# A transformer block on one core: where the second norm's factor enters, how wide the w_ada sums are, and when they run

## The chip, the core and the metric

One core of a Trainium2 chip runs the whole kernel. The time is device microseconds of one execution, the median of three runs. Engines are named as in the profile: PE multiplies matrices, PEld loads its stationary operand, DVE is the vector engine, ACT the scalar engine, POOL and SP here mostly issue transfers.

## What is computed

One block with batch 1, 256 rows (SEQ), 2048 columns (D), everything in float32:

```python
mod = silu(c) @ w_ada + b_ada                      # 6 vectors of 2048
sh1, sc1, g1, sh2, sc2, g2 = split(mod, 6)
h = rms_norm(x, norm_mix_g) * (1 + sc1) + sh1
u, q, k, v, ga, gb = split(h @ w_in)               # 8192 columns
merged = sigmoid(ga) * (s5(u) @ w_proj_ssm) + sigmoid(gb) * (attention(q, k, v) @ w_proj_attn)
x = x + g1 * (merged @ w_out)
h2 = rms_norm(x, norm_mlp_g) * (1 + sc2) + sh2
x = x + g2 * (square(relu(h2 @ w_ff1)) @ w_ff2)    # 8192 hidden
return rms_norm(x, norm_final_g)
```

`s5` is a state-space scan over the rows with a GLU (`w_glu`) behind it.

## The kernel before

**Weights.** Each float32 product is made of three products of a shorter type (hi by hi, hi by lo, lo by hi). Weights come in 456 tiles of 128x1024 (512 KB): `load` (L133 to L141) issues the transfer on SP into one of seven `wraw` buffers, and `split` (L143) makes the high part `whi` by an ACT cast (L145) and the low part `wlo` by a DVE subtract (L147), each with four buffers. In order: 80 tiles of w_in for q, k, v and u, woven with the first groups of the gate columns; 48 for the gates `ga`, `gb`; 8 of w_proj_attn, 8 of w_glu, 8 of w_proj_attn, 16 of w_proj_ssm, 32 of w_out, then ff1 and ff2. `stream` hands the tiles to three forms of product: `gemm_t` (L177 to L179, 24 matmuls of 128x256 a tile, transposed result `pt`), `gemm_d` (L194 and L196, result `pd`) and `gemm_n` (L218 to L220, 12 of 128x512, result `pn`). Matmul results share five banks ("mm"), small ones three ("ax").

**Side work.** After each weight tile `step` runs the jobs of the lanes, each lane with a rate in jobs per tile (R1, R2, RS0, RWO, RM and so on). The order on each engine is then set by a scheduler that simulates the program; `hot` and high priority move parts of it ahead, and `after` keeps an instruction behind another one. The lane that matters here is "ada": the vectors of `mod` are row sums of the transposed w_ada times silu(c). One sum is a load of 128x1024 and one DVE instruction with an accumulator (L279). The scale and shift of the first norm come first: 48 such sums for rows 4 to 15 of its 16 (`mod1`, into a ring of `ahm` tiles), in pairs of 128-row blocks, each pair with its part of the normed input (`make_h1`: `htmp`, `ah`) behind it. Next come 96 sums, "late", for the second norm's scale and shift (A2, B2) and the gate g1, through the `wraw` buffers; last 32 for g2 during ff1 and ff2.

**Attention and scan.** When u is complete it goes over POOL's queue into another layout (`hop_in`, L743), and POOL then loads the table `tz` of attention's position terms (L441). Attention's first step on DVE reads scores and `tz` (`ga<-sco,tz`, L694). Scan and gating follow in lane "m".

**The second norm.** Behind w_out, four banks at a time are multiplied by g1 (L1168), added to x (L1169) and squared with a sum on ACT (L1170); L1185 and L373 to L378 give the factor `rs2` of each row. `scale2` multiplies x by it (L1177, L1180), `make_h` transposes (`trh`, L669), applies A2 and B2 on ACT (`htmp`, L681) and splits into `h2h`. The first four units g of ff1 (`pt`, 1024 columns each) start with the first half of the rows (8 tiles by `gemm_t`), whose results ACT copies into `part` (L1282); the second half is added by `gemm_d`, and ReLU, square and split follow (L1229, L1230).

## Time and profile before

| what | value |
|---|---|
| median of three runs | 1422.48 us (1420.78 to 1424.05) |
| the profiled execution | 1422.84 us |
| its span | 1421.0 us |
| PE busy | 1376.6 us (97%) |
| DVE busy | 1057.4 us (74%) |
| ACT busy | 700.4 us (49%) |
| transfers | 354.52 MB, mean 249 GB/s |

A span is from the first to the last instruction; the rest of the execution lies around it. Matmuls are pipelined, so a PE that is called busy can still be fed slowly, and the time lost is best read from the distance of one matmul's start to the next. Rows of the timeline give start and duration in us, engine, line, operation, output and input tiles, and in brackets the idle time before it and what ended it.

### The profile page before, as it was taken

The page shows a single profiled execution, that of the slowest core. Times are in us where ns is not written, and L with a number is a line of the kernel's source. Part 1 is how long each engine was busy: PE and PEld are TensorE (multiplying, and loading weights), DVE is VectorE, ACT ScalarE, POOL GpSimd, SP SyncE. Part 2 cuts the span into 40 slices and gives each one's busy share as a digit, 9 for nine tenths or more (in the row PEclk, how much of TensorE's full clock was granted, in tenths as well). Part 3 has the DMA queues.
Part 4 walks back from the last instruction along what each step waited for, and adds up shares of the span by engine and source line. Part 5 has one row for each costly group of instructions (what it writes and reads, how often), then busy time and mean ns, then how long its engine had stood idle before and what let it go on. Part 6 is the DMA issues. An engine that isn't in the chain of part 4 may idle for free.

```text
span 1421.0 us, 24325 instructions
## 1 busy us (share of the span) xinstructions
PE 1376.6 (97%) x9716; PEld 1245.0 (88%) x9716; DVE 1057.4 (74%) x1517; ACT 700.4 (49%) x919; POOL 42.5 (3%) x95
## 2 busy tenths in 40 slices
PE   6999989999999999999899999999999999999996
PEld 5899989989899999988799988888888888888885
DVE  5798998876899788977686686778666555555676
ACT  4554434346645743345555554635363544634444
POOL 1000000400002200000000000000000000000000
PEclk9999999999999999999899999999999999999998
DMA  9999965795447999787598568788778666566551
GB/s 372 408 376 327 317 228 174 228 298 193 140 161 245 320 336 321 290 332 258 183 344 291 176 230 255 257 231 328 203 275 264 214 191 193 177 207 191 181 206 60
DMA packets 111346, 354.52 MB, mean 249 GB/s; under 512 B 12176, under 2 KB 12208, under 8 KB 110816
## 3 DMA queue, kind: packets, MB, share of 16 engines
q1 hardware_dynamic: 108336, 347.13, 71.9%
q0 software_dynamic: 2896, 5.83, 1.4%
q8 instruction: 76, 1.25, 0.4%
q14 instruction: 38, 0.31, 0.1%
HBM read 348.70 MB, written 2.51 MB: 247 GB/s over the span
## 4 chain that ended last, share of the span: by engine, by line
PE 87%; DVE 6%; DMA 3%; ACT 2%; issue 2%; SPq 0%; DVEq 0%; ACTq 0%
PE pd L194 12%; PE pn L218 11%; PE pn L219 11%; PE pn L220 11%; PE pt L177 11%; PE pt L178 10%; PE pt L179 10%; PE pd L196 6%; DVE wlo L147 2%; DMA wraw<-in_w_in_dram 2%; DVE wraw L279 1%; ACT whi L145 1%; PE trv L603 1%; DMA wraw<-in_w_proj_attn_dram 1%; PE rk L637 1%
## 5 line engine op out<-in xcount | busy, mean ns | idle before, releaser
L145 ACT CAST whi<-wraw 128x1024 fp32r<-128x1024 f32 x456 | 473.8, 1050 | 574.2 <-PE pt L178 189.5
L147 DVE TENSOR_TENSOR wlo<-wraw,whi 128x1024 fp32r<-128x1024 f32 x456 | 553.7, 1224 | 268.6 <-ACT whi L145 261.8
L194 PE MATMUL pd<-h2h,whi 128*128 128x512 f32 x768 | 265.9, 395 | 0.4 <-DVE part L1224 0.4
L177 PE MATMUL pt<-ah,whi 128*128 128x256 f32 x896 | 252.2, 289 | 10.2 <-ACT ah L145 8.1
L178 PE MATMUL pt<-ah,whi 128*128 128x256 f32 x896 | 252.9, 286 | 0.0
L179 PE MATMUL pt<-ah,wlo 128*128 128x256 f32 x896 | 246.7, 286 | 6.2 <-DVE wlo L147 6.2
L196 PE MATMUL pd<-h2h,wlo 128*128 128x256 f32 x768 | 208.1, 279 | 0.0
L219 PE MATMUL pn<-whi,ff 128*128 128x512 f32 x512 | 199.3, 389 | 0.0
L218 PE MATMUL pn<-whi,ff 128*128 128x512 f32 x512 | 198.2, 389 | 0.0
L177 PEld LDWEIGHTS pt<-ah,whi 128*128 128x128 f32 x896 | 171.4, 193 | 12.9 <-ACT ah L145 9.0
L220 PE MATMUL pn<-wlo,ff 128*128 128x512 f32 x512 | 182.4, 389 | 0.0
L179 PEld LDWEIGHTS pt<-ah,wlo 128*128 128x128 f32 x896 | 169.3, 193 | 7.7 <-DVE wlo L147 7.4
L178 PEld LDWEIGHTS pt<-ah,whi 128*128 128x128 f32 x896 | 173.3, 193 | 1.5 <-issue 0.8
L194 PEld LDWEIGHTS pd<-h2h,whi 128*128 128x128 f32 x768 | 142.2, 188 | 31.7 <-issue 0.7
L279 DVE SCALAR_TENSOR_TENSOR wraw<-wraw,cb 128x1024 f32<-128x1024 f32 x128 | 155.9, 1220 | 0.0
L196 PEld LDWEIGHTS pd<-h2h,wlo 128*128 128x128 f32 x768 | 144.7, 188 | 3.1
L218 PEld LDWEIGHTS pn<-whi,ff 128*128 128x128 f32 x512 | 96.1, 188 | 20.3 <-issue 0.2
L220 PEld LDWEIGHTS pn<-wlo,ff 128*128 128x128 f32 x512 | 96.1, 188 | 20.0
L219 PEld LDWEIGHTS pn<-whi,ff 128*128 128x128 f32 x512 | 96.1, 188 | 19.6
L177 PE MATMUL pt<-h2h,whi 128*128 128x256 f32 x256 | 72.5, 288 | 1.1 <-ACT h2h L145 1.1
L178 PE MATMUL pt<-h2h,whi 128*128 128x256 f32 x256 | 73.1, 287 | 0.0
L179 PE MATMUL pt<-h2h,wlo 128*128 128x256 f32 x256 | 72.2, 288 | 0.0
(347 smaller groups left out, 1840.2 us busy)
## 6 DMA issues: line engine op xcount, KB each, us to landing
wraw<-in_w_ff_dram SPq DMA_DIRECT2D x256, 512.0 KB, 5.0
wraw<-in_w_in_dram SPq DMA_DIRECT2D x128, 512.0 KB, 5.7
wraw<-in_wat_dram SPq DMA_DIRECT2D x128, 512.0 KB, 5.6
ahm<-in_wat_dram SPq DMA_DIRECT2D x48, 512.0 KB, 7.0
wraw<-in_w_out_dram SPq DMA_DIRECT2D x32, 512.0 KB, 6.4
wraw<-in_w_proj_attn_dram SPq DMA_DIRECT2D x16, 512.0 KB, 6.4
wraw<-in_w_proj_ssm_dram SPq DMA_DIRECT2D x16, 512.0 KB, 5.5
ahm<-in_wan_dram SPq DMA_DIRECT2D x8, 512.0 KB, 10.9
```

The source lines that it names most:

```text
L145: h = self.nc.scalar.copy(hi, src)
L147: s = self.nc.vector.tensor_sub(lo, src, hi.bitcast(F32))
L177: nc.tensor.matmul(o, hi[:, c], xh[:, kx, :], start=st, stop=False, skip_group_check=True)
L178: nc.tensor.matmul(o, hi[:, c], xl[:, kx, :], start=False, stop=False, skip_group_check=True)
L179: self.mm = nc.tensor.matmul(o, lo[:, c], xh[:, kx, :], start=False, stop=sp, skip_group_check=True)
L194: nc.tensor.matmul(banks[blk], hi[:, c], x2[:, :, kt, :], start=i + k == 0, stop=False, skip_group_check=True)
L196: self.mm = nc.tensor.matmul(banks[blk][:, S:2 * S], lo[:, c], x2[:, 0, kt, :], start=False, stop=i == n - 1 and k == 1, skip_group_check= ...
L218: nc.tensor.matmul(o, xh[:, kx, tk], hi[:, c], start=q == 0, stop=False)
L219: nc.tensor.matmul(o, xl[:, kx, tk], hi[:, c], start=False, stop=False)
L220: self.mm = last = nc.tensor.matmul(o, xh[:, kx, tk], lo[:, c], start=False, stop=q == n - 1)
L279: v.scalar_tensor_tensor(w, w, 1.0, self.cb[:, (i % 2) * 1024:(i % 2 + 1) * 1024], op0=OP.mult, op1=OP.mult, accum_out=pc[:, i:i + 1])
L603: nc.tensor.matmul(p[q, k * 64:(k + 1) * 64], self.VT[q, i, 8 * b + k, :], self.ident[q, q], start=True, stop=True)
```

## The change

**1. The second norm's factor enters the first unit at its evacuation.** The factor `rs2` is one number for each row of x, so it can be applied behind the product. For the first four 128-row blocks of unit g = 0, `make_h` works on the unnormed x1 times A2, without factor and without shift, giving `hp`; that runs in a lane during the second half of w_out. Their four weight tiles are split into homes of their own (`wf`, in slots VT and QT), and the unit's products run from `hp` and `wf`. `h_first` and `h_second`, called at its third and fourth tile, make the normed `h2h` of blocks 0 to 7 for the other units and a broadcast R of the factor (`rrow`). DVE evacuates the unit's banks with a product by R (`part<-pt,R`). The missing shift (B2 of four blocks times the first 512 rows of those w_ff1 columns) is summed by DVE from four loads of an additional layout `w1t` (`shift_job`) and enters as bias of ReLU. The second part of unit 0 begins at block 4 instead of 8.

**2. Sums over rows of 2048 columns.** In `mod1` one DVE instruction of 128x2048 (`ada_wide`) stands for two of 128x1024 and the add behind them; the loads remain of 128x1024.

**3. The second modulation's sums run later.** The rates of the ada lane change; g1 comes ahead of the later parts of A2 and B2; in unit g = 0 the lane rests. Loads of w_ada on SP by the weights around them: 49 before and 48 now up to weight 60; 11 and 7 from 60 to 84; 38 and 31 from 84 to 152; 12 and 13 in w_proj_ssm (152 to 168); 15 and 24 in w_out (168 to 200); 19 and 22 in the first four units of ff1 (200 to 232).

The diff, cut to its core:

```diff
-R1 = 1.65
-R2 = .8
...
+R1 = .92
+R2 = .45
...
-RWO = .45
-RM = .72
+RWO = .75
+RM = .98
...
+    def stream(self, src, kts, c0, homes=()):
+        homes = list(homes)
         for kt in kts:
             with self.tc.high_priority(offset=OFF):
                 w = self.load(src, kt, c0)
-                hi = self.wp.tile([P, 1024], F32R, name="whi", tag="whi", bufs=4)
-                lo = self.wp.tile([P, 1024], F32R, name="wlo", tag="wlo", bufs=4)
+                if homes:
+                    hi, lo = homes.pop(0)
+                else:
+                    hi = self.wp.tile([P, 1024], F32R, name="whi", tag="whi", bufs=4)
+                    lo = self.wp.tile([P, 1024], F32R, name="wlo", tag="wlo", bufs=4)
...
+    def gemm_t(self, src, kts, c0, xh, xl, koff=0, mid={}, homes=()):
         nc = self.nc
         banks = [self.bank(f"pt{b}") for b in range(4)]
         n = len(kts)
-        for i, (kt, hi, lo) in enumerate(self.stream(src, kts, c0)):
+        for i, (kt, hi, lo) in enumerate(self.stream(src, kts, c0, homes)):
             kx = kt - koff
-            if mid and i == n // 2:
-                mid()
+            if i in mid:
+                mid[i]()
...
+    def shift_job(self, row, wb):
+        nc, v = self.nc, self.nc.vector
+        st = {}
+
+        def load(i):
+            w = st[i] = self.wp.tile([P, 1024], F32, name="wraw", tag="wraw", bufs=7)
+            with self.after(self.last):
+                nc.sync.dma_start(w, self.a["w1t"][i])
+
+        def total(i):
+            w = st.pop(i)
+            for k in range(2):
+                q = w[:, k * 512:(k + 1) * 512]
+                with self.after(self.agate or self.done[-1][0]):
+                    v.scalar_tensor_tensor(q, q, 1.0, row, op0=OP.mult, op1=OP.mult,
+                                           accum_out=wb[:, 2 * i + k:2 * i + k + 1])
+        return [(lambda i=i: load(i), lambda i=i: total(i)) for i in range(4)]
+
+    def ada_wide(self, vec, k0, n, done, ring):
+        nc, v = self.nc, self.nc.vector
+        pc = self.cp.tile([P, n], F32, name="pw", tag=f"pw{n}", bufs=3)
+        st = {}
+
+        def load(i):
+            w = st[i] = ring.pop(0)
+            r0 = vec * D + (k0 + i) * P
+            for h in range(2):
+                with self.after(self.last):
+                    nc.sync.dma_start(w[:, h * 1024:(h + 1) * 1024],
+                                      self.a["wat"][r0:r0 + P, h * 1024:(h + 1) * 1024])
+
+        def total(i):
+            w = st.pop(i)
+            with self.after(self.done[-1][0]):
+                v.scalar_tensor_tensor(w, w, 1.0, self.cb, op0=OP.mult, op1=OP.mult, accum_out=pc[:, i:i + 1])
+            if i == n - 1:
+                done(pc)
+        return [(lambda i=i: load(i), lambda i=i: total(i)) for i in range(n)]
...
+    def make_h(self, x, kts, A, B, gate=None, to=None):
+        nc = self.nc
+        self.h_lo = []
+        ah, al = to or (self.ah, self.al)
         for ks in self.pairs(kts):
             p = self.tmp("trh")
             for k, kt in enumerate(ks):
                 for t in range(2):
-                    self.nc.tensor.transpose(p[:, k * S + t * P:k * S + (t + 1) * P],
-                                             x[:, t, kt * P:(kt + 1) * P], self.ident)
-            yield p
-
-    def make_h(self, x, kts, A, B, pre=None):
-        nc = self.nc
-        self.h_lo = []
-        pre = iter(pre or self.make_h_t(x, kts))
-        for ks in self.pairs(kts):
-            p = next(pre)
+                    with self.after(gate):
+                        nc.tensor.transpose(p[:, k * S + t * P:k * S + (t + 1) * P],
+                                            x[:, t, kt * P:(kt + 1) * P], self.ident)
             h = self.big.tile([P, 2, S], F32, name="htmp", tag="htmp", bufs=1)
             for k, kt in enumerate(ks):
-                nc.scalar.activation(h[:, k, :], p[:, k * S:(k + 1) * S], AF.Identity,
-                                     scale=A[:, kt:kt + 1], bias=B[:, kt:kt + 1])
+                if B is None:
+                    nc.scalar.activation(h[:, k, :], p[:, k * S:(k + 1) * S], AF.Copy, scale=A[:, kt:kt + 1])
+                else:
+                    nc.scalar.activation(h[:, k, :], p[:, k * S:(k + 1) * S], AF.Identity,
+                                         scale=A[:, kt:kt + 1], bias=B[:, kt:kt + 1])
...
+            self.h_lo.append(self.split(ah[:, o, :], al[:, o, :], h[:, 0:len(ks), :]))
...
-            return (self.ada_job(1, k0, n, fin_scale(1, A1, lambda: self.gmix, k0, n), ring)
-                    + self.ada_job(0, k0, n, fin_shift(0, B1, k0, n), ring))
+            return (self.ada_wide(1, k0, n, fin_scale(1, A1, lambda: self.gmix, k0, n), ring)
+                    + self.ada_wide(0, k0, n, fin_shift(0, B1, k0, n), ring))
...
-        late = self.ahead(mod2(0) + mod2(1) + sum([self.ada_job(2, 4 * ch, 4, fin_g1(ch)) for ch in range(4)], [])
-                          + mod2(2) + mod2(3))
+        late = self.ahead(mod2(0) + sum([self.ada_job(2, 4 * ch, 4, fin_g1(ch)) for ch in range(4)], [])
+                          + mod2(1) + mod2(2) + mod2(3))
...
+        wide = [h[:, 2 * i:2 * i + 2, :].rearrange("p k c -> p (k c)") for h in (hv, hq) for i in range(2)]
+        ring = wide * 3 + wide[2:4] * 6
...
-        free = {None: range(8)}
-        free.update({i: (i + 8,) for i in range(16)})
-        free.update({i: (i + 4,) for i in range(20, 44)})
+        free = {None: range(4)}
+        free.update({i: (i + 4,) for i in range(8)})
+        free.update({i: (i + 2,) for i in range(10, 22)})
...
-        self.lanes["ada"][1] = RPA
+        self.lanes["ada"][1] = RS2
...
         proj_attn(0)
+        self.lanes["ada"][1] = RPA
...
+                hp = self.slot("T", [P, 2, 4, S], F32R, name="hp")
+                self.lane("hp", [lambda k0=k0: self.make_h(x1, range(k0, k0 + 2), A2, None, self.mm, (hp[:, 0], hp[:, 1]))
+                                 for k0 in (0, 2)], .25)
             self.flush("x", "g1")
+            if cg:
+                self.flush("hp")
...
-            s0 = scale2(0, 1, None)
-            self.make_h(xs, range(0, 4), A2, B2)
-            h0 = self.h_lo[0]
-            scale2(1, 0, h0)
-            self.make_h(xs, range(4, 8), A2, B2)
-            h1 = self.h_lo[1]
-        self.gates = [(s0, None)] * NS + [(s0, self.sq_last)] * (2 - NS) + [(h0, self.sq_last)] * 2
-        self.agate = h1
+            s0 = scale2(0, 0, None)
+            s1 = scale2(1, 0, s0)
+        self.gates = [(None, None)] * 4 + [(s1, self.sq_last)] * 2
+        self.agate = s1
+        b2r = self.slot("RT", [P, 512], name="b2r")
+        wb = self.col("wb", 8)
+        hs = {}
+
+        def h_first():
+            with self.hot():
+                self.make_h(xs, range(0, 4), A2, B2, self.mm)
+                hs["h0"] = self.h_lo[-1]
+
+        def h_second():
+            with self.hot():
+                p = self.aux("rrow")
+                for t in range(2):
+                    with self.after(self.mm):
+                        nc.tensor.matmul(p[:, t * P:(t + 1) * P], rs2[:, t:t + 1].to_broadcast([P, P]), self.ident,
+                                         start=True, stop=True)
+                nc.scalar.copy(self.R, p[:, 0:S])
+                self.make_h(xs, range(4, 8), A2, B2, self.mm)
+                hs["h1"] = self.agate = self.h_lo[-1]
+                self.gates += [self.done[-1]] * 2
...
+                    if g:
+                        nc.scalar.activation(t[:, b], t[:, b], AF.Relu)
+                    else:
+                        for k in range(2):
+                            q = t[:, b, k * S:(k + 1) * S]
+                            nc.scalar.activation(q, q, AF.Relu, bias=wb[:, 2 * b + k:2 * b + k + 1])
...
-        self.lanes["ada"][1] = RM
+        self.lanes["ada"][1] = 0.0
         for g in range(NP):
             part = self.slot(("S4", "T", "SV", "S5")[g], [P, 4, 512], name="part")
-            banks = self.gemm_t(w1, range(0, 8), g * 1024, self.ah, self.al)
+            if g:
+                banks = self.gemm_t(w1, range(0, 8), g * 1024, self.ah, self.al)
+            else:
+                wh, wl = [self.slot(n, [P, 4, 1024], F32R, name="wf") for n in ("VT", "QT")]
+                banks = self.gemm_t(w1, range(0, 4), 0, hp[:, 0], hp[:, 1], mid={2: h_first, 3: h_second},
+                                    homes=[(wh[:, k, :], wl[:, k, :]) for k in range(4)])
             for b in range(4):
-                nc.scalar.copy(part[:, b, :], banks[b])
+                if g:
+                    nc.scalar.copy(part[:, b, :], banks[b])
+                else:
+                    with self.after(hs["h0"]):
+                        v.tensor_mul(part[:, b, :].rearrange("p (k s) -> p k s", s=S),
+                                     banks[b].rearrange("p (k s) -> p k s", s=S),
+                                     self.R[:, None, :].to_broadcast([P, 2, S]))
             parts.append(part)
             if g == 0:
-                self.gates = []
+                self.lanes["ada"][1] = RM
                 self.agate = None
-                scale2(2, 0, h1)
-                scale2(3, 0, h1)
+            if g == 1:
+                scale2(2, 0, self.done[-1][0])
+                scale2(3, 0, self.done[-1][0])
+                self.ada_bcast(B2[:, 0:4], b2r, self.mm)
         self.flush()
+        self.lane("shift", self.ahead(self.shift_job(b2r, wb)), .34)
...
-                ff1(g, 8, parts[g])
+                ff1(g, 8 if g else 4, parts[g])
...
+            "w1t": f("w_ff1")[0:512, 0:1024].T.reshape(4, 2, P, 512).transpose(0, 2, 1, 3).reshape(4, P, 1024),
```

How the order of instructions changes, at three places. First PE, from the last product of w_out to the first of the normed input; `pn` is w_out's result, `mh` its input. Before:

```order
L218 MATMUL pn_7427<-whi,mh 128x512
L219 MATMUL pn_7427<-whi,mh 128x512
L220 MATMUL pn_7427<-wlo,mh 128x512
L669 MATMUL trh<-ident,xs 128x128 x8
L177 MATMUL pt_7820<-h2h,whi 128x256
```

And of the changed kernel, where 86 more rows of products of `hp` and `wf` stand in the place of the first dots and six in that of the second:

```order
L224 MATMUL pn_7359<-wlo,mh 128x512
L181 MATMUL pt_7751<-hp,wf 128x256
...
L181 MATMUL pt_7753<-hp,wf 128x256
L182 MATMUL pt_7753<-hp,wf 128x256
L716 MATMUL trh<-ident,xs 128x128 x2
L1256 MATMUL rrow<-ident,r2s 128x128
L716 MATMUL trh<-ident,xs 128x128 x6
L1256 MATMUL rrow<-ident,r2s 128x128
L183 MATMUL pt_7753<-hp,wf 128x256
...
L716 MATMUL trh<-ident,xs 128x128 x8
L181 MATMUL pt_7916<-h2h,whi 128x256
```

Between w_out and the transposes 89 products have come to stand, and the transposes of the first eight blocks follow each other closely. Next DVE at the same place, from the factor on. Before:

```order
L378 SCALAR_TENSOR_TENSOR r2s<-r2t,r2s 128x2
L1180 TENSOR_SCALAR xs<-x,r2s 128x512
L147 TENSOR_TENSOR wlo<-wraw,whi 128x1024 x2
L147 TENSOR_TENSOR h2h<-htmp,h2h 128x512
L1180 TENSOR_SCALAR xs<-x,r2s 128x512 x2
L147 TENSOR_TENSOR wlo<-wraw,whi 128x1024 x2
L147 TENSOR_TENSOR h2h<-htmp,h2h 128x512
```

And of the changed kernel:

```order
L421 SCALAR_TENSOR_TENSOR r2s<-r2t,r2s 128x2
L1229 TENSOR_SCALAR xs<-x,r2s 128x512 x4
L147 TENSOR_TENSOR wlo<-wraw,whi 128x1024
L283 SCALAR_TENSOR_TENSOR wraw,pc<-wraw,cb 128x1024
L147 TENSOR_TENSOR wlo<-wraw,whi 128x1024
L283 SCALAR_TENSOR_TENSOR wraw,pc<-wraw,cb 128x1024
L147 TENSOR_TENSOR h2h<-htmp,h2h 128x512 x2
L1361 TENSOR_TENSOR part<-pt_7751,R 128x512
L1361 TENSOR_TENSOR part<-pt_7752,R 128x512
L1361 TENSOR_TENSOR part<-pt_7753,R 128x512
L1361 TENSOR_TENSOR part<-pt_7754,R 128x512
L147 TENSOR_TENSOR h2h<-htmp,h2h 128x512 x2
```

All four scalings stand together, two weight splits and two sums follow, and the evacuation of unit 0 stands between two pairs of `h2h` subtracts. Last, DVE at the last pair of the first norm, blocks 14 and 15; the last `ah<-htmp` is that pair's subtract, `ahm` holds rows of w_ada, `B_114` is the shift. Before:

```order
L147 TENSOR_TENSOR wlo<-wraw,whi 128x1024
L279 SCALAR_TENSOR_TENSOR ahm,pc<-ahm,cb 128x1024
L874 SCALAR_TENSOR_TENSOR A_113<-A_113,cols 128x2
L147 TENSOR_TENSOR wlo<-wraw,whi 128x1024
L279 SCALAR_TENSOR_TENSOR ahm,pc<-ahm,cb 128x1024
L283 TENSOR_TENSOR pcs<-pc 128x2
L879 TENSOR_TENSOR B_114<-pcs,cols 128x2
L147 TENSOR_TENSOR ah<-htmp,ah 128x512
```

And of the changed kernel:

```order
L325 SCALAR_TENSOR_TENSOR ahm,pw<-ahm,cb 128x2048
L147 TENSOR_TENSOR wlo<-wraw,whi 128x1024
L610 TENSOR_TENSOR tt<-bp,AB 128x512
L611 TENSOR_TENSOR tt<-bp,AB 128x512
L147 TENSOR_TENSOR wlo<-wraw,whi 128x1024
L921 TENSOR_TENSOR B_114<-pw,cols 128x2
L147 TENSOR_TENSOR wlo<-wraw,whi 128x1024
L611 TENSOR_TENSOR bp<-tt 128x32x16
L147 TENSOR_TENSOR wlo<-wraw,whi 128x1024
L147 TENSOR_TENSOR ah<-htmp,ah 128x512
```

The last sum has moved away from the pair's subtract: four weight splits and the scan's preparation (`tt`, `bp`) stand between them now, and the shift is added two splits ahead of the subtract.

20 lines of the change are left out of this document (7 added, 13 removed).

## The prediction

> **What bounds the kernel now.** I read the page first, then PE's waits, then busy time by stretch, and last the timeline at the places where PE waits. From the page, the span, the busy time of the engines' first row and the chain:
>
> ```profile
> span 1421.0 us, 24325 instructions
> PE 1376.6 (97%) x9716; PEld 1245.0 (88%) x9716; DVE 1057.4 (74%) x1517; ACT 700.4 (49%) x919; POOL 42.5 (3%) x95
> PE 87%; DVE 6%; DMA 3%; ACT 2%; issue 2%; SPq 0%; DVEq 0%; ACTq 0%
> ```
>
> TensorE (PE) is the bound: 87% of the chain is its matmuls, and the change alters their number very little. What can be won are the places where PE waits. PE's waits, each with total, count and longest in us (those of the first 50 us, which the change leaves alone, and the small ones left out):
>
> ```profile
> PE pt L177 <- ACT ah L145: 8.1, 5, 3.6
> PE pt L179 <- DVE wlo L147: 6.2, 5, 2.4
> PE trh L669 <- DVE xs L1180: 4.3, 1, 4.3
> ...
> PE pt L177 <- ACT gb L1101: 1.9, 1, 1.9
> ```
>
> Some of the `ah` waits lie in the first 50 us too. The longest single one behind it is the second norm (4.3). The stretches that the sum needs; columns: span, its length, busy time of PE, PEld, DVE, ACT, POOL, granted clock of PE, DMA share, GB/s:
>
> ```profile
> 50.00:100.00 50.00, 49.05 (x364) 46.72 (x363) 48.96 (x78) 28.93 (x40) 0.00 (x0) 1.00 1.03 406
> 200.00:205.00 5.00, 2.94 (x13) 2.94 (x14) 2.96 (x3) 1.98 (x4) 0.00 (x0) 0.69 0.18 70
> 300.00:305.00 5.00, 4.24 (x23) 4.04 (x23) 5.00 (x7) 0.97 (x1) 0.00 (x0) 0.66 0.84 327
> 480.00:485.00 5.00, 4.63 (x26) 4.63 (x27) 2.74 (x3) 4.94 (x8) 0.00 (x0) 0.68 0.98 392
> 600.00:690.00 90.00, 86.91 (x395) 71.97 (x393) 67.78 (x91) 42.18 (x57) 0.00 (x0) 1.00 0.78 280
> 720.00:750.00 30.00, 29.90 (x250) 29.70 (x250) 24.05 (x32) 17.62 (x26) 0.00 (x0) 1.00 0.96 354
> ```
>
> To see: three short stretches outside the norm run at a granted clock of .66 to .69 right behind a wait, and the weight stages with few waits already move 280 to 406 GB/s. Now the norm itself, from the timeline (start, duration, engine, line, output<-input, count, idle before it):
>
> ```profile
> 686.30 0.39 PE L219 MATMUL pn<-whi,mh 128*128 128x512 f32 x1
> 686.52 0.39 PE L220 MATMUL pn<-wlo,mh 128*128 128x512 f32 x1
> ...
> 690.38 0.16 DVE L378 SCALAR_TENSOR_TENSOR r2s<-r2t,r2s 128x2 f32<-128x2 f32 x1
> 690.58 0.49 DVE L1180 TENSOR_SCALAR xs<-x,r2s 128x512 f32<-128x512 f32 x1
> ...
> 691.21 0.66 PE L669 MATMUL trh<-ident,xs 128*128 128x128 f32 x2 [4.30 <-DVE xs L1180]
> ...
> 693.26 1.02 ACT L681 ACTIVATE htmp<-trh,B,A 128x256 f32<-128x256 f32 x2 [0.99 <-PE trh L669]
> 694.31 0.62 ACT L145 CAST h2h<-htmp 128x512 fp32r<-128x512 f32 x1
> 694.96 0.69 DVE L147 TENSOR_TENSOR h2h<-htmp,h2h 128x512 fp32r<-128x512 f32 x1 [1.62 <-ACT h2h L145]
> 694.98 1.22 PE L177 MATMUL pt<-h2h,whi 128*128 128x256 f32 x4 [1.12 <-ACT h2h L145]
> ...
> 700.05 1.11 PE L669 MATMUL trh<-ident,xs 128*128 128x128 f32 x8
> ```
>
> The last matmul of w_out starts at 686.52; then come sums of squares, factor, scaling, transposes, modulation and split, one behind the other, and PE has nothing else. From 694.98 its matmuls stand 0.213 us apart (23 of them from 694.98 to 700.05, the first four in one row), against 0.12 where the clock is full, as at 198 us:
>
> ```profile
> 198.45 0.28 PE L178 MATMUL pt<-ah,whi 128*128 128x256 f32 x1
> 198.57 0.28 PE L179 MATMUL pt<-ah,wlo 128*128 128x256 f32 x1
> 202.06 1.22 PE L177 MATMUL pt<-ah,whi 128*128 128x256 f32 x4 [3.21 <-ACT ah L145]
> ```
>
> **Term 1, the second norm.** What it costs now: 686.52 to 700.05 is 13.53 us, in which one w_out matmul (0.22 by the spacing of the first two rows), 8 transposes (1.11 for the eight at 700.05, of which the last one's drain is some 0.25: 0.11 each) and 23 matmuls at 0.12 were issued, 3.9 us of work; 9.65 us are lost. After the change 96 matmuls on unnormed `hp` against weights kept in `wf` are there to fill it: 96 x 0.12 = 11.5 us. In the new order 89 stand ahead of the first transpose, so PE is supplied until 686.75 + 10.7 = 697.4. The factor exists at 690.5 and does not depend on the removed filler; the four scalings (0.49 each) end near 692.6 even on DVE alone, so the transposes find their data. Behind them stand 7 more `hp` matmuls and 8 transposes, to about 700.2. The first h2h tile needs transposes (698.1), two activations (1.02), a cast (0.62), a subtract (0.69): 700.5. So the norm itself is covered. What is late next is the bank: with five for matmuls, the next unit has one free and gets the others when DVE has done `part<-pt,R` (0.69 each), which stand behind two h2h subtracts on DVE. I take 1.5 us for that wait (between 0 and 3.5: two subtracts and two products in a row, 2.8, and the activation before them).
>
> Added PE work: 8 more transposes (0.87), two row matmuls for the factor (0.22) and four that broadcast the shift (0.11 each if they stand as close as the transposes, twice that and more if not: 0.4 to 1.1). Four weight tiles change to the form with fewer and longer matmuls for the same product, counted as nothing. Together 1.5 to 2.2; I take 1.9. DVE gets 8 shift sums and ACT 4 activations more in stages where DVE is at 24.05 of 30 us and PE waits for neither: nothing, or some tenths should a split queue behind them. Gain 9.7 - 1.5 - 1.9 = **6.3** (3 to 7.8).
>
> A rule bears on the new gap. Behind an earlier wait of some 2 us the clock fell:
>
> ```profile
> 478.22 0.28 PE L177 MATMUL pt<-yh,whi 128*128 128x256 f32 x1
> 480.37 0.39 PE L177 MATMUL pt<-yh,whi 128*128 128x256 f32 x1 [1.88 <-ACT gb L1101]
> ...
> 481.81 0.41 PE L179 MATMUL pt<-yh,wlo 128*128 128x256 f32 x1
> 482.02 0.42 PE L178 MATMUL pt<-yl,whi 128*128 128x256 f32 x1
> ```
>
> From 481.81 matmuls stand 0.21 apart, and the stretch 480 to 485 has the clock at .68: a third of 5 us is lost, 1.6, though PE had idled only 1.88 us. So a wait of 1.5 us need not be free of it, and 1.5 us more stand in the low end of term 1. The Trainium skill, "TensorE: Matmul & The Clock Gate", Part 1, has the clock halved only after an idle window of about 3.4 us; by it no extra end would stand there. The row at 480.37 disagrees with that, so I keep the end.
>
> **Term 2, the last pair of the first norm.** PE stops at 198.57 and goes on at 202.06: 3.4 us beyond spacing; clock .69 over 5 us costs 1.5 more; two small waits ahead some 1.0. Lost: 5.9. Now the last wide sum stands after 54 weight splits, not among 56 to 58, and its shift is added after 56; the pair's subtract keeps its place. DVE also does less:
>
> ```profile
> L279 DVE SCALAR_TENSOR_TENSOR ahm<-ahm,cb 128x1024 f32<-128x1024 f32 x48 | 57.9, 1224 | 0.0
> L279 DVE DVE_READ_ACCUMULATOR wraw<-wraw,cb 128x1 f32 x128 | 10.8, 85 | 0.0
> ```
>
> A sum of 1024 columns is 1.224 + 0.085. One of 2048 isn't in the trace; two of 1024 less one fixed part (0.69 for 512 columns and 1.224 for 1024 give 0.156 fixed) is 2.29, at worst 2.45. So 24 wide sums save 24 x (2 x 1.309 - 2.29 - 0.085) = 5.8 us of DVE, 2 at worst, in a stage where DVE is busy 48.96 of 50 us. Two DVE steps earlier (2.4 and more) do not quite cover 3.4, the shorter queue does the rest: gain **4.5** (1.5 to 5.9).
>
> **Term 3, the start of attention.** Here weights land late:
>
> ```profile
> 297.63 0.28 PE L179 MATMUL pt<-ah,wlo 128*128 128x256 f32 x1
> 299.74 0.38 PE L177 MATMUL pt<-ah,whi 128*128 128x256 f32 x1 [1.83 <-ACT whi L145]
> ...
> 301.00 0.58 PE L179 MATMUL pt<-ah,wlo 128*128 128x256 f32 x1 [0.76 <-DVE wlo L147]
> ```
>
> The table `tz` that attention waits for (its last issue on POOL, the group of its four transfers with the median landing), and the first step on DVE that reads it:
>
> ```profile
> 285.89 0.49 POOL L441 DMA_DIRECT2D tz<-scr  x1 [0.33 <-DMA u<-uT]
> tz<-scr POOLq DMA_DIRECT2D x4, 256.0 KB, 10.0
> 305.53 0.39 DVE L694 SCALAR_TENSOR_TENSOR ga<-sco,tz 128x128 f32<-128x128 f32 x1
> ```
>
> Lost: 2.0 behind 297.63, 0.9 at 301.00 (the wait and the filling of PE behind it), and 1.7 by the clock (.66 of 5 us). The lower rate puts 7 loads of w_ada between weights 60 and 84 where 11 stood, each 512 KB at that spot. Against it: attention's first step on DVE (`ga<-sco,tz`) now stands six splits earlier, while `tz` lands at about 296 (285.89 + 10). Six weights of PE's 2.8 us before 305.53 is about 289: DVE may wait up to 7 us there, with its splits queued behind, and PE behind those. Up to four split weights (`whi`, `wlo` have four buffers) cover 11 us where they are full, but here loads are late and they are not. Gain **2.5** (-2 to 4.6).
>
> **Terms 4 to 6, DVE further on.** Of the 6.2 us for `wlo`, 0.8 each are the small waits at 198 and 301 and 0.9 lie in the first stage; the other two, 3.8 with a longest of 2.4, lie at 370 to 430, where scan and splits share DVE; the new order puts ten operations, not 13, between the two splits there: **2** (0 to 3.8). At 478 us 3.6 are lost (2.0 wait, 1.6 clock), behind copies that were late on ACT; six sums, not twelve, stand on DVE around it: **2** (0 to 3.6). In the first stage the pair of rows 8 and 9 gets its last wide sum two splits later and its subtract three: **-1.4** (-3, about that many splits of 1.22 uncovered, to 0).
>
> **Term 7, what the moved sums cost.** Sums are taken from the front and put behind the scan: w_out carries 24 loads of w_ada, not 15, and the first four units of ff1 22, not 19, of which 20 stand one beside each weight.
>
> ```profile
> ACT whi L145 <- DMA wraw<-in_w_out_dram: 27.4, 16, 4.4
> wraw<-in_w_out_dram SPq DMA_DIRECT2D x32, 512.0 KB, 6.4
> ```
>
> 32 w_out weights take 32 x 12 matmuls at 0.22 to 0.23, 87 us of PE; 56 loads of 0.524 MB in that is 338 GB/s, where 47 gave 283 (the trace: 280). DVE goes from 67.78 by nine sums of 1.3 and two splits to 81 of 90. 354 GB/s was reached without loss at 720 to 750, 406 in the first stage. But ACT already waits 27.4 us for these loads without PE noticing; that reserve shrinks. **-3** (-10 to 0) for w_out and ff1 together. The ends come from the rival below and from the 720 to 750 row. The Trainium skill, "DMA: Bandwidth & Descriptors", Specifications, gives 358 GB/s as one core's share of HBM; ff1's demand there (40 loads in 20 x 2.88 us, 364 GB/s) would then cost about 1 us more. The 406 of 50 to 100 us is above that figure, so I don't count it.
>
> **Sum.** 6.3 + 4.5 + 2.5 + 2 + 2 - 1.4 - 3 = 12.9. The profiled execution took 1422.84 us (span 1421.0 and 1.84 around it); 1422.84 - 12.9 = 1409.9. It lies 0.36 above the median of 1422.48; on the median's scale 1409.6.
>
> **Rivals.**
> - *Seven buffers become the bound* (slower). Each load holds one of seven `wraw` buffers from issue to the end of its subtract: 6.4 landing, cast 1.05, subtract 1.22, in all 8.7 plus queueing. With 56 loads in 87.2 us the stay may be 7 x 87/56 = 10.9 us. If busier DMA and DVE make it 12.0, w_out takes 56 x 12/7 = 96 us, 9 more, and the 20 weights of ff1 with their 20 sums 40 x 12/7 = 68.6 for 57.6, 11 more: 20 lost against 15.9 gained in terms 1 to 6, 1426.6. The signs change at a stay of 11.7. For it: 27.4 us of waits for loads. Against: 720 to 750 holds 354 GB/s with the same seven buffers. 0.07.
> - *The front's stalls only move.* Terms 2 to 6 sum to nothing, since DVE there is full and `tz` sets attention's start: 1422.5 - 6.3 + 3 = 1419.2. For it: 48.96 of 50 us. 0.12.
> - *The norm's cover fails.* `hp` and `wf` must be split by DVE between the evacuations of w_out, on a DVE at 90%; if they come late PE waits there instead, and term 1 is nought: 1422.5 - 6.6 = 1415.9. 0.13.
> - *Everything at its better end*, loads free: below 1405. 0.08.
>
> **How the numbers follow.** The forecast has the remaining 0.60, 1405 to 1414.5. The range 1403 to 1418.5 leaves out the first rival, about half of the second, and the tail below: two in ten. About 0.2% (2.8 us) is what a measurement of this kernel can tell from no change. Faster by more is below 1419.6: 0.60 + 0.13 + 0.08 + half the second rival, 0.87; same: the other half, 0.06; slower: 0.07.
>
> **What would show it.** In the changed profile: no wait of PE at `trh` behind w_out, `pt<-hp,wf` in its place, clock 1.0 over 690 to 720, and a wait below 2 us on `part`; PE's `ah` wait at 198 gone; the stretch 295 to 305 with a shorter wait, or one whose releaser is a split held by `ga<-sco,tz`; 600 to 690 near 340 GB/s with PE at 100%. PE waiting for `whi` or `wlo` in w_out or ff1 would make the prediction wrong, and so would a wait on `hp`.

## The result and the profile after

The changed kernel takes 1412.35 us (median of 4, 1412.14 to 1413.22) against 1423.26 for the kernel before in the same comparison: ratio 0.9921, 95% interval 0.9908 to 0.9935. That is 10.9 us less; 12.9 were forecast. The profiled execution took 1412.14 us. Its page, with span, first row of busy times and chain:

```profile
span 1410.4 us, 24298 instructions
PE 1376.1 (98%) x9704; PEld 1241.2 (88%) x9704; DVE 1062.2 (75%) x1480; ACT 704.3 (50%) x926; POOL 42.5 (3%) x95
PE 90%; DVE 5%; DMA 2%; ACT 1%; issue 1%; DVEq 0%; SPq 0%; ACTq 0%
```

PE's waits in the changed kernel (those at `ss` in the first 50 us and the small ones left out), and, from 185 to 215 us alone, what is left of the `ah` wait at 198:

```profile
PE pt L181 <- ACT ah L145: 5.7, 5, 3.2
PE pt L183 <- DVE wlo L147: 3.7, 2, 3.3
PE pn L222 <- ACT whi L145: 1.5, 3, 0.8
PE pt L181 <- DVE part L1361: 1.5, 1, 1.5
PE pd L200 <- DVE wlo L147: 1.0, 1, 1.0
...
PE pt L181 <- ACT ah L145: 1.1, 1, 1.1
```

The wait of the transposes for `xs` and the one for `gb` are gone. New are one of 3.3 for `wlo`, one of 1.5 for `part`, and small ones in w_out (`pn`) and ff1 (`pd`). The rest of the `ah` waits, 4.6 us, lies in the first 50 us. The stretches that belong to these waits:

```profile
108.00:113.00 5.00, 1.67 (x12) 1.47 (x12) 5.00 (x8) 2.76 (x4) 0.00 (x0) 0.87 1.00 355
113.00:118.00 5.00, 5.00 (x25) 5.00 (x25) 3.88 (x4) 0.00 (x0) 0.00 (x0) 0.50 1.01 381
300.00:305.00 5.00, 5.00 (x44) 5.00 (x44) 5.00 (x9) 3.15 (x7) 0.00 (x0) 1.00 0.94 350
480.00:485.00 5.00, 5.00 (x44) 5.00 (x43) 4.12 (x7) 4.05 (x5) 0.00 (x0) 1.00 0.83 205
600.00:690.00 90.00, 88.16 (x428) 72.76 (x427) 78.87 (x117) 42.34 (x57) 0.00 (x0) 1.00 0.91 334
690.00:720.00 30.00, 27.74 (x227) 26.93 (x226) 23.42 (x36) 14.73 (x22) 0.00 (x0) 1.00 0.70 250
800.00:820.00 20.00, 18.16 (x103) 15.41 (x103) 16.40 (x27) 11.34 (x17) 0.00 (x0) 1.00 0.78 291
```

At 300 and 480 PE has full work at full clock where it had .66 and .68. At 113 to 118 it now runs at half clock. The norm, from the timeline:

```profile
679.31 0.39 PE L224 MATMUL pn<-wlo,mh 128*128 128x512 f32 x1
...
679.53 0.28 PE L181 MATMUL pt<-hp,wf 128*128 128x256 f32 x1
...
685.63 0.16 DVE L421 SCALAR_TENSOR_TENSOR r2s<-r2t,r2s 128x2 f32<-128x2 f32 x1
...
690.21 0.38 PE L716 MATMUL trh<-ident,xs 128*128 128x128 f32 x2
...
695.05 0.28 PE L183 MATMUL pt<-h2h,wlo 128*128 128x256 f32 x1
696.05 2.48 DVE L1361 TENSOR_TENSOR part<-pt,R 128x512 f32<-128x512 f32 x4
696.78 0.38 PE L181 MATMUL pt<-h2h,whi 128*128 128x256 f32 x1 [1.45 <-DVE part L1361]
```

`hp` products follow w_out at once and last until the transposes, 4.6 us behind the factor (685.63). What is late next is the bank: 1.45 us for `part`.

The stages one by one. The table gives the start of the last matmul of a weight tile in the timeline (a tile counted along PE as 24 matmuls of `pt`, 12 of `pn` or 16 of `pd`), as a difference in us from the kernel before; negative is earlier. Runs: part 1 alone (norm), part 3 alone (moves), all but part 2 (first), and a better version (mix_a); they are told below. Tile 48 is in the first stage, 84 at attention's start, 128 ends the gates, 152 w_proj_attn and w_glu, 200 w_out; 264 ends the first part of ff2.

| tile | before | changed | norm | moves | first | mix_a |
|---|---|---|---|---|---|---|
| 24 | 110.09 | -1.5 | +0.6 | 0.0 | -0.1 | -0.7 |
| 48 | 178.27 | +5.9 | +0.6 | 0.0 | -0.1 | +5.7 |
| 84 | 312.24 | -1.5 | +0.4 | -3.3 | -4.6 | -1.7 |
| 104 | 394.71 | -6.5 | +0.5 | -4.7 | -6.0 | -6.7 |
| 128 | 477.02 | -8.1 | +0.4 | -5.1 | -6.5 | -8.3 |
| 152 | 549.75 | -11.7 | +0.5 | -8.8 | -10.1 | -11.9 |
| 200 | 686.52 | -7.2 | +3.5 | -3.2 | -6.2 | -11.0 |
| 208 | 722.46 | -14.5 | -6.5 | -1.0 | -12.9 | -20.2 |
| 232 | 792.32 | -13.1 | -0.9 | -0.6 | -11.2 | -17.7 |
| 264 | 881.02 | -10.8 | +2.1 | -0.6 | -8.8 | -16.9 |
| last | 1409.56 | -10.7 | +2.2 | -0.6 | -8.7 | -16.9 |

The count goes by weights alone, and PE's other matmuls can stand ahead of a tile in one kernel and behind it in another. It matters in row 84: there the changed kernel and mix_a have already issued 14 matmuls of attention, 1.9 us of PE (tiles 83 and 84 take 3.20 and 4.51 us where a tile without other work takes 2.88), that the others issue behind it. With the same work done the changed kernel is 3.4 us ahead there, not 1.5. From row 104 to row 152 all columns have the same other work behind them.

Repeated executions of one kernel spread over up to 6.6 us (the kernel before, 1418.44 to 1425.03 in one comparison), so a single profile's last row is less sure than a median. Stages where two kernels run the same instructions in the same order mostly agree within some tenths, but not always: moves and first have PE's order in common up to 640 us and differ by 1.3 us from tile 60 on.

### The profile page after: what moved, and what is told of

It reads as the page before. It is cut to its first block, busy times and chain, and to the rows that moved or that the text cites. A ratio compares the mean times of both kernels' runs of the same rounds, so it can differ in the third digit from the quotient of the medians.

```text
span 1410.4 us, 24298 instructions
## 1 busy us (share of the span) xinstructions
PE 1376.1 (98%) x9704; PEld 1241.2 (88%) x9704; DVE 1062.2 (75%) x1480; ACT 704.3 (50%) x926; POOL 42.5 (3%) x95
## 4 chain that ended last, share of the span: by engine, by line
PE 90%; DVE 5%; DMA 2%; ACT 1%; issue 1%; DVEq 0%; SPq 0%; ACTq 0%
PE pt L181 12%; PE pd L198 12%; PE pt L182 12%; PE pt L183 12%; PE pn L222 10%; PE pn L223 10%; PE pn L224 10%; PE pd L200 6%; DVE wlo L147 2%; DMA wraw<-in_w_out_dram 1%; DVE wraw L283 1%; PE trv L646 1%; ACT whi L145 1%; PE ys L864 1%; PE rk L680 1%
## 5 line engine op out<-in xcount | busy, mean ns | idle before, releaser
L198 PE MATMUL pd<-h2h,whi 128*128 128x512 f32 x800 | 277.0, 396 | 0.9 <-ACT whi L145 0.9
L200 PE MATMUL pd<-h2h,wlo 128*128 128x256 f32 x800 | 216.3, 280 | 1.0 <-DVE wlo L147 1.0
L198 PEld LDWEIGHTS pd<-h2h,whi 128*128 128x128 f32 x800 | 148.1, 188 | 33.3 <-ACT whi L145 1.2
L283 DVE SCALAR_TENSOR_TENSOR wraw<-wraw,cb 128x1024 f32<-128x1024 f32 x128 | 156.1, 1220 | 0.0
L200 PEld LDWEIGHTS pd<-h2h,wlo 128*128 128x128 f32 x800 | 150.8, 188 | 5.2 <-DVE wlo L147 1.7
L325 DVE SCALAR_TENSOR_TENSOR ahm<-ahm,cb 128x2048 f32<-128x2048 f32 x24 | 55.0, 2290 | 0.0
L181 PE MATMUL pt<-h2h,whi 128*128 128x256 f32 x192 | 52.6, 286 | 2.0 <-DVE part L1361 1.5
L182 PE MATMUL pt<-h2h,whi 128*128 128x256 f32 x192 | 52.3, 283 | 0.2 <-DVE h2h L147 0.2
```

What stands on the lines that cost most here:

```text
L181: nc.tensor.matmul(o, hi[:, c], xh[:, kx, :], start=st, stop=False, skip_group_check=True)
L182: nc.tensor.matmul(o, hi[:, c], xl[:, kx, :], start=False, stop=False, skip_group_check=True)
L198: nc.tensor.matmul(banks[blk], hi[:, c], x2[:, :, kt, :], start=i + k == 0, stop=False, skip_group_check=True)
L200: self.mm = nc.tensor.matmul(banks[blk][:, S:2 * S], lo[:, c], x2[:, 0, kt, :], start=False, stop=i == n - 1 and k == 1, skip_group_check= ...
L283: v.scalar_tensor_tensor(w, w, 1.0, self.cb[:, (i % 2) * 1024:(i % 2 + 1) * 1024], op0=OP.mult, op1=OP.mult, accum_out=pc[:, i:i + 1])
L325: v.scalar_tensor_tensor(w, w, 1.0, self.cb, op0=OP.mult, op1=OP.mult, accum_out=pc[:, i:i + 1])
```

## The experiments

**Part 1 alone (norm).** The changed kernel with sums of 1024 columns, the old rates and the old order of late sums:

```diff
-R1 = .92
+R1 = 1.65
...
-RWO = .75
-RM = .98
+RWO = .45
+RM = .72
```

> The kernel before with part 1 of the change alone: old rates of the sums (R1 to RM), old order of the late sums, sums of 1024 columns. Theory: the waits of the norm go by themselves. Between the last product of w_out and full speed PE then loses 3 to 4 us where it lost 9.65, and does 1.9 us more work (transposes, rows, broadcast); the first stage, the stops at 198, 297, 374 and 478 stay as before. Gain 4 to 5.5 us, so a ratio of 0.996 to 0.997. Rival: hp and wf are only in time because the sums were moved; then PE waits at hp, and the ratio is 0.999 to 1.002.

Measured: 1422.52 us, ratio 1.0001 (0.9989 to 1.0013). The gain at the norm is all there, even larger: 9.9 us from tile 200 to 208, and PE is busy nearly all of 690 to 720. It is lost again by tile 248. That stretch, and the timeline where the fourth unit of ff1 ends:

```profile
690.00:720.00 30.00, 29.77 (x245) 29.25 (x244) 24.67 (x41) 16.59 (x29) 0.00 (x0) 1.00 0.50 174
...
774.48 0.28 PE L183 MATMUL pt<-h2h,wlo 128*128 128x256 f32 x1
774.60 1.47 PE L716 MATMUL trh<-ident,xs 128*128 128x128 f32 x12
777.19 0.66 PE L716 MATMUL trh<-ident,xs 128*128 128x128 f32 x4 [1.12 <-ACT htmp L723]
778.57 0.50 PE L198 MATMUL pd<-h2h,whi 128*128 128x512 f32 x1 [0.72 <-DVE h2h L147]
```

The 16 transposes of blocks 8 to 15 stand in one heap behind the unit, and PE then waits for activation, cast and subtract block by block: the norm's chain over again, in small. Both theories missed: the ratio is the rival's, but PE does not wait on `hp`, and the gain of the first theory comes and goes again. By w_out's end the run is 3.5 us behind. Of this 0.9 is the `hp` transposes; 2.0 was lost in w_proj_ssm, where norm_early below, with the same order of PE's instructions, lost nothing: that part is scatter between executions, and this profile's execution took 1425.06 us, 2.5 above the run's median.

**With the late rates (norm_rates).** The late rates of the change on top of the run before:

```diff
-RPA = .75
-RWO = .45
-RM = .72
+RPA = .85
+RWO = .75
+RM = .98
```

> The run with part 1 alone, plus the three late rates of the change (RPA .85, RWO .75, RM .98); the front as before. Theory (part 1 alone gained nothing because the lane of sums rests in unit 0, so that the last shift of the second modulation comes at 771 us as before and PE waits for it and for what queues behind it): the last B2 is ready before PE's fourth unit ends; of the 8.6 us that part 1 alone lost between 716 and 840, over 5 come back; total 1416 to 1418. Rival (the loss there comes from the eight more products in the other form, the shift sums and their loads): the loss stays within 2 us of 8.6, total 1421 to 1424.

Measured: 1429.39 us, one run. The last shift is ready at 731.6 us, not 771, and still the transposes stand behind the unit, from 780.9. Tiles 224 to 232 took 26.9 us, 28.5 in part 1 alone, 22.7 in the changed kernel. So the theory of a late shift fell. The rival's size held (6.9 us lost from tile 208 to 248, where part 1 alone lost 8.6), its total did not. What is left is the order, which the next run tests. By w_out's end, with more sums in it, this run is 3.1 us later than part 1 alone.

**One block group earlier (norm_early).** Part 1 alone again, with the input of blocks 8 to 11 made in the fourth unit:

```diff
+                h8 = {2: lambda: self.make_h(xs, range(8, 12), A2, B2)} if g == 3 else {}
-                banks = self.gemm_t(w1, range(0, 8), g * 1024, self.ah, self.al)
+                banks = self.gemm_t(w1, range(0, 8), g * 1024, self.ah, self.al, mid=h8)
...
-        for c in (2, 3):
+        for c in (3,):
```

> The run with part 1 alone, with one move: the normed input of blocks 8 to 11 is made in the fourth unit of ff1 (at its third tile) and not behind it; blocks 12 to 15 stay behind. Theory (part 1 alone loses again between 716 and 790 because all 16 transposes stand behind the fourth unit and PE waits for activation, cast and subtract in turn, though their data was ready; faster sums did not help): at least 4 of the 5.8 us that the stretch of tiles 224 to 232 took longer than in the changed kernel come back; total 1417 to 1420. Rival (the loss comes from the late last shift, at 771 us): blocks 12 to 15 wait for it all the same, under 2 us come back.

Measured: 1419.04 us, one run, beside 1423.85 (1419.52 to 1425.41). Tiles 224 to 232 take 23.5 us, 5.0 less, and the last matmul comes 3.8 us earlier than before. At its own place the order of the transposes is thus shown to be the loss. What it is worth in all is less sure: PE's order is the same as in part 1 alone up to 750 us, and yet this run is already 2.8 us ahead of it at the end of w_out; behind w_out it gains 3.2 on it. Part 1 alone is worth some 1 to 4 us if the second half of the normed input is woven into the unit ahead, as the scheduler did by itself in the changed kernel (there its transposes lie at 720 to 745). Why it chose otherwise under the old rates stays open.

**Part 3 alone (moves).** The kernel before with the new rates from R3 on and the new order of late sums.

```diff
-RWO = .45
-RM = .72
+RWO = .75
+RM = .98
```

> The kernel before with part 3 of the change alone: the new rates from R3 to RM and the new order of the late sums; R1, R2, the sums of 1024 columns and the norm stay as before. Theory (the waits between 290 and 490 go because fewer late sums stand there): no stop over 1.5 us at 297 and 478, w_proj_ssm begins 10 us earlier than before; w_out gives back 2 to 4 us, the norm costs its 9.65 us; total 6 to 7 us faster, ratio 0.995 to 0.996. Rival (the front's gain needs the shorter first stage of the wide sums): the stops only move, ratio 0.998 to 1.001.

Measured: 1421.81 us, ratio 0.9997 (0.9984 to 1.001). The stops at 297 and 478 are gone and w_proj_ssm begins 8.8 us earlier, as the theory has it. But by the end of w_out 5.6 of it is given back, more than the 2 to 4 expected (1.5 of it in w_proj_ssm, where 14 matmuls that broadcast g1 stand that were in w_out before), and the norm costs 2.2 more than before. The ratio is the rival's. PE's waits from 600 to 720:

```profile
PE trh L669 <- DVE xs L1181: 5.2, 2, 4.3
PE pn L218 <- ACT whi L145: 3.1, 2, 2.2
```

Neither part alone gains; together (first, below) they are 8.7 us ahead by the profile, and the one run of 1413.9 us lies below all 13 of the kernel before beside it (1419.28 to 1424.67).

**The first stage.** `old_first` is the changed kernel with the first stage of before; `narrow_rate` is the same with R1 1.84 and R2 .9; `wide_fast` is the changed kernel with R1 1.1 and nothing else.

```diff
-            return (self.ada_wide(1, k0, n, fin_scale(1, A1, lambda: self.gmix, k0, n), ring)
+            return (self.ada_job(1, k0, n, fin_scale(1, A1, lambda: self.gmix, k0, n), ring)
...
-R1 = .92
-R2 = .45
+R1 = 1.65
+R2 = .8
```

> The changed kernel with the first stage of before: sums of 1024 columns, ring of eight homes, R1 1.65, R2 .8; the rest of the change stays. Theory (the wide sums make the new stop at 108 us): no stop of PE for wlo at 108, so 6 us less between 100 and 120 with the half clock; the stop for ah at 198 comes back, 5 to 6 us with its half clock; the total is that of the changed kernel within 1.5 us. Rival (the stop at 108 comes from what else moved): PE waits 3 us for wlo at 108 here too, and the total is 5 us longer than the changed kernel's.

> The changed kernel with sums of 1024 columns and twice the rates (R1 1.84, R2 .9), so that as many bytes are summed for each weight as with wide sums. Theory 'width': a sum of 2.29 us holds up the splits behind it, and two of 1.22 let a split in between; no stop over 1 us at 108 here. Theory 'rate': the sums of the pair of rows 8 and 9 come too thick or too late for DVE at this rate, whatever their width; the stop of about 3 us with its half clock stays. The extra 5.8 us of DVE time of narrow sums speaks for more stops, not fewer, in the second theory.

> The changed kernel with R1 1.1 in place of .92: wide sums that start a fifth earlier by weights. Theory 'late': the shift of rows 8 and 9 is ready late and DVE catches up at one spot; with an earlier start the stop at 108 falls below 1 us, and the total falls by 4 to 6 us to about 1407. Theory 'width or load': DVE is full anyway, and sums put in earlier hold up splits earlier: the stop moves ahead of 108 or stays, total within 2 us of the changed kernel.

Measured: 1413.9, 1412.72 and 1422.7 us, one run each. Narrow sums have no stop at 108 at either rate, so the stop belongs to the wide sums with their four homes and not to the rate. The stretch in `narrow_rate`, and the changed kernel at that place:

```profile
108.00:118.00 10.00, 10.00 (x85) 9.99 (x84) 9.28 (x12) 7.27 (x11) 0.39 (x1) 1.00 0.94 342
...
107.09 2.29 DVE L325 SCALAR_TENSOR_TENSOR ahm<-ahm,cb 128x2048 f32<-128x2048 f32 x1
...
108.78 0.28 PE L182 MATMUL pt<-ah,whi 128*128 128x256 f32 x1
109.30 0.08 DVE L325 DVE_READ_ACCUMULATOR ahm<-ahm,cb 128x1 f32 x1
109.30 1.22 DVE L147 TENSOR_TENSOR wlo<-wraw,whi 128x1024 fp32r<-128x1024 f32 x1
...
111.11 1.22 DVE L147 TENSOR_TENSOR wlo<-wraw,whi 128x1024 fp32r<-128x1024 f32 x1
...
112.39 0.58 PE L183 MATMUL pt<-ah,wlo 128*128 128x256 f32 x1 [3.33 <-DVE wlo L147]
```

One sum of 2.29 us holds back two splits, and PE stops. But narrow sums bring the stop at 198 back (3.2 us; 4.4 in `narrow_rate`): the two forms lose at different places. At tile 128, with the same work done, the changed kernel, `old_first` and `narrow_rate` stand at -8.1, -6.5 and -8.1. That is no difference beyond the scatter (moves, with the PE order of `old_first`, stands 1.3 behind it), so the runs do not show that the width of these sums sets the time at all.

`wide_fast` has no wait for `wlo` at 108 any more; PE waits there 1.1 and 0.6 us for `ah`, and 2.7 us are lost in that tile. It is 5.0 us ahead at tile 84 with the same work done as before (the 8 at tile 88 that an expectation below names include 19 matmuls of attention that it had yet to issue), then loses all of it, in the main at 370 and 422:

```profile
PE pt L183 <- DVE wlo L147: 6.0, 2, 3.9
```

The stop shrank, not quite to the 1 us of the theory 'late', and the total is 10 us longer, so both theories fail for the total.

**W_out.** The sums queued during w_out take 32 of 1024 columns:

```diff
-                v.scalar_tensor_tensor(w, w, 1.0, self.cb[:, (i % 2) * 1024:(i % 2 + 1) * 1024], op0=OP.mult,
+                m = 32 if self.cheap else 1024
+                v.scalar_tensor_tensor(w[:, 0:m], w[:, 0:m], 1.0, self.cb[:, (i % 2) * 1024:(i % 2) * 1024 + m],
```

> The changed kernel, but the sums of w_ada that are queued during w_out take 32 columns of each tile in place of 1024 (this part of the modulation is left out); all loads stay. Theory 'buffers and DMA' (rival of the prediction in small): PE's stops in w_out, 3.8 us at 600 to 640, come from loads that land late; they stay over 2 us, since the loads are as many. Theory 'DVE': splits and evacuations queue behind the sums on DVE; without them the stops fall below 1 us and w_out is 3 us shorter. A buffer is also freed 1.2 us earlier here, so a fall below 1 us alone does not tell a late split from a late buffer; what PE and ACT wait for tells it.

Measured: 1412.11 us, one run. The stretch 600 to 690, ACT's wait for loads from 600 to 680, and, last, the same wait in the changed kernel:

```profile
600.00:690.00 90.00, 90.00 (x458) 76.64 (x457) 58.02 (x113) 44.49 (x62) 0.00 (x0) 1.00 0.92 340
ACT whi L146 <- DMA wraw<-in_w_out_dram: 29.0, 17, 4.3
...
ACT whi L145 <- DMA wraw<-in_w_out_dram: 30.1, 15, 4.8
```

No stop is left with as many loads, 340 GB/s and nearly the same waits of ACT. So the transfers' rate is not what stops PE in w_out; the sums' 1.22 us on DVE are, through splits behind them or buffers freed later, which this run does not part. The 2.4 us gained by tile 200 are gone by tile 248: PE then waits 2.6 us for `wlo` in unit 0.

**Unit 0 without the shift sums (no_shift).** `shift_job` is left out, its result set to zero:

```diff
-        self.lane("shift", self.ahead(self.shift_job(b2r, wb)), .34)
+        v.memset(wb, 0.0)
```

> The changed kernel without the shift sums: their four loads and eight DVE instructions are gone and the bias of unit 0's ReLU is zero (this part is left out). Theory: the stop of 2.3 us at 809 to 812, in the second part of unit 0, comes from them: DVE holds a load's buffer until the sums, and the weights behind land late; without them the stop is below 0.7 us and the total 1.5 to 2.5 us shorter. Rival: it comes from the sums of the last modulation vector, which start there at the same time; then the stop stays within 0.7 us.

Measured: 1409.49 us, one run. The stretch 800 to 820 here, and DVE and PE around the stop in the changed kernel (L305 a shift sum, L283 one of the last modulation vector):

```profile
800.00:820.00 20.00, 20.00 (x117) 17.49 (x116) 14.70 (x22) 11.74 (x17) 0.00 (x0) 1.00 0.69 231
...
805.02 0.68 DVE L305 SCALAR_TENSOR_TENSOR wraw<-wraw,b2r 128x512 f32<-128x512 f32 x1
...
808.51 1.22 DVE L283 SCALAR_TENSOR_TENSOR wraw<-wraw,cb 128x1024 f32<-128x1024 f32 x1
...
810.98 1.22 DVE L147 TENSOR_TENSOR wlo<-wraw,whi 128x1024 fp32r<-128x1024 f32 x1
...
812.25 0.39 PE L200 MATMUL pd<-h2h,wlo 128*128 128x256 f32 x1 [0.97 <-DVE wlo L147]
```

PE has no stop here, and the last matmul comes 2.8 us earlier than in the changed kernel. That is what the shift sums cost beside the sums of the last modulation vector, which stand among them on DVE. mix_a below keeps the shift sums, lets the others begin later, and idles 0.5 us there: it seems that taking either away is enough.

**Better versions (mix_a, mix_b, mix_narrow).** mix_a has four edits to the changed kernel, three of them here:

```diff
-RS2 = .3
-RWO = .75
+RS2 = .55
+RWO = .6
...
-                    with self.after(hs["h0"]):
...
-        self.lane("ada", late2, 0.3)
+        self.lane("ada", late2, 0.0)
...
             if i == 1:
+                self.lanes["ada"][1] = 0.3
```

The fourth makes the input of blocks 8 to 15 inside the fourth unit, as norm_early does for 8 to 11. mix_b also has another front (R1 1.1, R4 .35, RS0 .4, RS1 .25, RS2 .75); mix_narrow is mix_a with the old first stage.

> The changed kernel with four edits that lie in different stages, each read at its own place: the product by R of unit 0 no longer stands behind the h2h subtracts (the 1.5 us wait for part falls below 0.7); RS2 .55 and RWO .6 (six sums more in w_proj_attn and the last gate unit, four fewer in w_out: PE's stops at 600 to 640 fall from 3.8 us to below 2); the normed input of blocks 8 to 15 is made in the fourth unit; and the sums of the last modulation vector start only behind unit 0 (the stop of 2.3 us at 809 falls below 1). Theory: 2 to 5 us faster than the changed kernel, ratio to before 0.989 to 0.991. Rival (loads and sums only push each other on): the stops come back in w_proj_ssm or ff1, ratio 0.992 to 0.994.

> As mix_a, with another front: R1 1.1, R4 .35, RS0 .4, RS1 .25, RS2 .75, so that wide sums start earlier and fewer late sums stand between 290 and 450. Theory (the run with R1 1.1 was 8 us ahead at tile 88 and lost it to splits that queued behind late sums beside attention and scan at 370 and 421): with fewer sums there it keeps at least 3 of the 8, ratio 0.986 to 0.989. Rival (scan and splits stand in each other's way there without sums too): the stops at 370 and 421 stay over 3 us together, and it is slower than mix_a.

> mix_a with part 2 of the change undone: sums of 1024 columns, eight homes, R1 1.65, R2 .8. It tells what the wide sums are worth in a version whose later stops are gone. Theory (they save DVE time, and DVE's arrears in the first stage are paid behind it, so a shorter queue is worth 1 to 3 us by the end of the gates though PE's stop at 198 only changes place with one at 108): the stop at 108 is gone, the one at 198 is back, PE is ahead of mix_a at 310 us and 1 to 3 us behind it at 490 and at the end; ratio 0.990 to 0.991. Rival (worth nothing): the same time as mix_a within 0.7 us.

Measured: mix_a 1406.52 us, ratio 0.9889 (0.9862 to 0.9915); mix_b 1405.97, 0.9884 (0.9861 to 0.9906); mix_narrow 1409.66, 0.9912 (0.989 to 0.9933). Of mix_a, w_out, the norm and unit 0:

```profile
600.00:690.00 90.00, 90.00 (x460) 76.86 (x459) 77.16 (x108) 44.26 (x63) 0.00 (x0) 1.00 0.89 327
685.00:715.00 30.00, 28.69 (x234) 27.88 (x233) 22.35 (x36) 14.02 (x21) 0.00 (x0) 1.00 0.69 240
800.00:820.00 20.00, 19.54 (x112) 16.86 (x111) 14.59 (x24) 11.27 (x15) 0.00 (x0) 1.00 0.71 244
```

Three of its edits show at their own place: no stop in w_out (3.5 us less from tile 168 to 200), no wait for `part` (a wait of 0.8 for `whi` in its place; 1.9 us less from 200 to 208), and 0.5 us in place of 1.8 idle at 800 to 820. The fourth brings nothing: tiles 208 to 232 take 1.1 us longer than in the changed kernel, which had those transposes woven in already. mix_a was not run beside the changed kernel; its four times all lie below that kernel's four, by the profiles it is 6.2 us ahead, and the intervals of the two ratios overlap. In mix_b the stops at 370 and 422 fall to 0.4 us in all, as the theory had it, and it is 2.4 us ahead of mix_a at tile 152. At 200 it is 0.6 ahead, with the same work done, and at 208 level, where PE waits 2.1 us for `whi` and `wlo`: of the 3 us expected nothing is left, though the stops did not come back as the rival had it. The time that the front wins does not reach the end here either. mix_narrow's profile is 1.7 us behind mix_a's and its median 3.1 above, from another comparison; the two intervals overlap, and code that is the same has differed by 1.3 us and more. Whether wide sums are worth anything in this version is not settled.

## Why the prediction was right, and where it was off

The direction and the size held, 10.9 us for 12.9, but by terms that were off both ways. By stages of the profile, forecast (the terms that lie there) and measured: to tile 48 +1.4 and +5.9 (term 6); 48 to 84 -7.0 and -9.3 (terms 2 and 3); 84 to 128 -2 and -4.7 (term 4); 128 to 152 -2 and -3.6 (term 5); 152 to 264 -3.3 and +0.9 (terms 1 and 7). The 14 attention matmuls ahead of tile 84 (1.9 us) are counted where the kernel before has them. Sums: -12.9 and, with 0.1 behind tile 264, -10.7. So the first stage lost 4.5 more than forecast, the stages from tile 48 to 152 won 6.6 more, and the rest missed its gain by 4.2. That the sum came out within 2.2 is in part luck.

- *Term 1, the norm.* The mechanism was right step by step: `hp` covers the chain, the factor is in time, the bank is late next, at 1.45 us for the 1.5 taken. The bound of 1.5 more for the clock was not needed: 690 to 720 stands at 1.00. With the small stops behind it PE loses 3.3 us up to tile 208, not 1.5, against 9.65. The added work of PE is 8 transposes, 4 row matmuls and 8 of the broadcast, not 8, two and four: 2.1 us by their spacing for the 1.9 taken. Mis-sized was the step that took the 8 shift sums on DVE at "nothing, or some tenths": beside the sums of the last vector they cost 2.8.
- *Term 6* was the worst: a loss of 1.4, bounded at 3, was 6.2 with the half clock behind the stop (113 to 118 at .50, which the bound left out, though term 2 had counted just that at 198).
- *Terms 2 and 3.* PE's `ah` wait at 198 fell from 3.2 to 1.1 us, with the clock at 1.00 behind it, and PE is full at 300 to 305; of the 10.5 us that the two terms counted as lost, 9.3 came back. The feared wait for `tz` did not show on PE.
- *Terms 4 and 5* were taken at about half of what was there to gain (3.8 and 3.6); all of it came, and 0.7 of a wait for `rw` in the scan with it.
- *Term 7.* W_out and ff1 lost more than the 3 taken, within the bounds: 4.5 from tile 152 to 200 (0.9 of it the transposes of `hp`), and the shift sums. PE's waits for `whi` in w_out (1.5 us) and for `whi` and `wlo` in ff1 (2.4 in all) are the sign that the prediction itself had named as making it wrong: here the term failed in small, at 334 GB/s and with PE at 98% where 100 was expected, without turning the sum. `w_out_cheap` shows the sums on DVE behind the waits in w_out, not the rate of transfers.
- *The second rival, stalls that only move,* is what the first stage did: most of the stop at 198 became one at 108. It did not hold for the stops from 297 to 478.
- *What the prediction did not see:* its terms were added as if independent. Parts 1 and 3 are worth nothing each by itself (ratios 1.0001 and 0.9997) and 8.7 us together by the profile. What part 3 wins in front, w_out and the norm take back; what part 1 wins at the norm, the next chain of transposes takes back unless it is woven in.

## What to carry to other kernels

Work that is moved out of the way of one stop has to be paid where it lands, so cost a change of rates as one sum over all stages, and try the parts apart before adding their gains: here two halves of nothing made 0.6%. Here the time won at one stop was often lost again at the next late chain, so look for the next place where transposes, activation, cast and subtract stand in a row behind a unit. An instruction of double width saves a fixed part on its engine but held up the short ones queued behind it; here that was no gain that the runs can tell from none. And compare stages of two kernels only where the same work lies behind both: a count by one kind of work alone had the changed kernel 1.9 us too late at tile 84.
